# V's scratch in a decoder block with dilated attention: dense by head pair, the first group laid out by partition

## The chip, the cores and the metric

The kernel runs on one core of a Trainium2 chip. A core has TensorE (PE; its weight loads are shown apart, as PEld), VectorE (DVE), ScalarE (ACT), GpSimd (POOL) and SyncE (SP), which here only issues transfers. Sixteen DMA engines move data between the chip's memory (HBM) and the core's on-chip memory (SBUF). The metric is the device time of one execution in microseconds, the median of the runs.

## The reference, cut to what matters

One layer with sequence 2048 and width 1024. A combined projection gives q, k and v for three groups of eight heads of 64, and the inputs of a second branch. Each group attends to keys at a stride; the three outputs of a head slot are combined by their softmax denominators.

```python
DILATION_GROUPS = ((128, 1), (512, 4), (2048, 16))
...
proj = x @ w_in[l] + b_in[l]
q, k, v, g_attn, u_lru, g_lru, gate_logits = jnp.split(proj, SPLIT_POINTS, axis=-1)
...
for g, (window, dilation) in enumerate(DILATION_GROUPS):
    o_g, lse_g = dilated_band_attention(q[:, :, g], k[:, :, g], v[:, :, g], window, dilation)
...
y_a = attn @ w_attn_proj[l]
...
y_b = (h * jax.nn.silu(g_lru)) @ w_lru_proj[l]
merged = gates[:, :, 0] * y_a + gates[:, :, 1] * y_b
out = merged @ w_out[l] + b_out[l]
x = layer_norm(DEEPNORM_ALPHA * x + out, ln_gain[l], ln_bias[l])
```

In the attention each residue class of positions modulo the stride is cut into blocks of 128 queries, and each block sees its own keys and, in the first two groups, those of the block before.

## The kernel before, in words

The work runs in stages, one after the other on TensorE. The **projection** (to about 1452 us) computes the 72 feature tiles of 128 columns in two halves of the sequence, each half two chunks of 512 positions. Most pairs of tiles are made by seven products instead of eight (a Strassen form); `MID` is the order of the seven, and the results become complete at products 5, 2, 4 and 3, in that order: second tile in the half's second chunk, first tile in its first chunk, second tile in its first chunk, first tile in its second chunk. Every operand is split into a high and a low part in a reduced float format, and three matmuls stand for one. The **attention** (1452 to about 1791 us) takes 12 units, a unit being one group and one pair of heads, in the order group 0, 2, 1 within a head pair. It runs in 48 steps of four blocks, and the second branch's output projection (`yb`) is interleaved with it. The **output** stage follows.

The order on every engine is written by hand: what a Python loop emits is what each engine's queue holds, in that order. In the projection small generators (`chains`) emit the steps of each result some products later.

V's way is this. `v_chain` (L359) takes a finished tile of V with features in partitions, turns its four blocks of 128 positions with TensorE (L366), and ScalarE copies them from PSUM into one of two buffers `vs` (L374). SyncE stores the buffer to the scratch in HBM (L378). There are 48 such stores, 12 tiles by four chunks. The scratch `v_scr` (L50) has a tensor for each group and each two head pairs, with 260 floats a row: 130 for each head pair, of which the first and the last hold ones, set once in the buffers (L354 to L356). Nothing reads the ones.

In the attention `v_parts` (L799) gives the four loads of a unit: four blocks of 128 keys each, into one half of the tile `V` (L806), so that two units are there at a time. Group 0 takes consecutive keys to a block (L809), group 1 takes every fourth (L811), group 2 every sixteenth (L813); a load has 512 rows of 128 floats. The loads of unit u + 1 are emitted in steps 4u + 1 and 4u + 2 (L1282); those of unit 0 near the end of the projection (L869), those of unit 1 in step 1 (L1269). `values` (L1020) multiplies V with the turned weights.

SyncE's queue also carries q and k of the next unit (`qk_parts`, L794), the second branch's state `hx` (L1176), which GpSimd splits in `split_h` (L1180, L1181) before TensorE uses it in `yb_part` (L1205), its weights `wlr` (L1155), and small tensors, among them the weights `wh` of the groups (L1122), which `spread` multiplies in at L1129.

Of the kernel before, what the change touches and what calls it, by code (L numbers as in the profile page):

```python
# [8 lines left out]
F32 = mybir.dt.float32  # L9
F32R = mybir.dt.float32r  # L10
AF = mybir.ActivationFunctionType
# [4 lines left out]
P = 128  # L16
S = 2048
# [3 lines left out]
CH = 512  # L21
HP = 4
# [9 lines left out]
def hybrid_block_kernel(ctx: ExitStack, tc: tile.TileContext, a: dict, out: bass.AP):  # L32
    nc = tc.nc
    sp, act, dve, pool, pe = nc.sync, nc.scalar, nc.vector, nc.gpsimd, nc.tensor

    def flat(t):
        return t.bitcast(F32)


    dram = ctx.enter_context(tc.tile_pool(name="dram", bufs=1, space=DRAM))  # L40
# [6 lines left out]
    mg_scr = dram.tile([2 * D, S], F32, name="mg_scr")  # L47
    yb_scr = dram.tile([D, S], F32, name="yb_scr")

    v_scr = [[dram.tile([S, 260], F32, name=f"v_scr{g}{j}") for j in range(2)] for g in range(3)]  # L50

    qk_scr = {(n, u): dram.tile([P, S], F32, name=f"{n}_scr{u}") for u in range(12) for n in ("q", "k")}

# [48 lines left out]
    def big(slot, shape, dt, name):  # L102
        return (cur["Z"] if slot[0] == "Z" else X).tile(shape, dt, name=name, tag=slot)
# [8 lines left out]
    def pe_later(lag, fn):  # L112
        pe_late.append((now["n"] + lag, fn))
# [26 lines left out]
    sl_p = stA.enter_context(tc.tile_pool(name="sl_p", bufs=1))  # L140
# [15 lines left out]
    def give(*ts):  # L156
        for t in ts:
            vacant.append(home.pop(id(t))[0])
# [191 lines left out]
        give_sent(rp)  # L350


    vs_free = [sl_p.tile([P, 4, 130], F32, name=f"vs{j}") for j in range(2)]
    for t in vs_free:  # L354
        dve.memset(t[:, :, 0:1], 1.0)
        dve.memset(t[:, :, 129:130], 1.0)  # L356
    tog = {"n": 0}

    def v_chain(vt, sgn, f, c):  # L359
        g, hp = divmod(f - FT_V, 4)  # L360
        st = {}

        def turn():
            tp = st["tp"] = ps.tile([P, 4, P], F32, tag="t", name=f"vtp{f}_{c}", bufs=2)
            for b in range(4):
                pe.transpose(tp[:, b, :], flat(vt)[:, b * P:(b + 1) * P], ident)  # L366
            give(vt)

        yield Ask(cond=lambda: tog["n"] < 2)
        tog["n"] += 1  # L370
        pe_later(2, turn)
        yield Ask(lag=3, cond=lambda: len(vs_free) > 0, ACT=.66)
        vs = vs_free.pop(0)
        act.activation(vs[:, :, 1:129], st["tp"], AF.Copy, scale=sgn)  # L374
        tog["n"] -= 1
        yield Ask()
        dst = v_scr[g][hp // 2][c * CH:(c + 1) * CH, (hp % 2) * 130:(hp % 2) * 130 + 130]
        sp.dma_start(dst.rearrange("(b p) f -> p b f", p=P), vs)  # L378
        vs_free.append(vs)


# [199 lines left out]
    def result(s, fi, c, bank, u):  # L581
# [10 lines left out]
        if kind in ("qk", "v"):  # L592
            y = take("y" + nm)
            total(flat(y), bank, u, f, sgn, True)
            start_chain(qk_chain(y, f, c) if kind == "qk" else v_chain(y, sgn, f, c))
        elif kind == "mg":
            y = take("y" + nm, F32)
            total(y, bank, u, f, sgn, False)
            start_chain(mg_chain(y, sgn, f, c))
        elif kind == "ga" or not fi:  # L600
            y = take("y" + nm, F32)
            total(y, bank, u, f, sgn, False)
            start_chain(silu_chain(y, sgn, f, c))
        else:
            i = f - FT_U
            if c == 1 and i in put_off:
                y = take("y" + nm, F32)
                total(y, bank, u, f, sgn, True)
                act.activation(ubs[:, i, 2, 0:3], y[:, CH - 3:CH], AF.Copy)
                start_chain(store_chain(y, u_scr[i]))  # L610
                return
            ub = ub_free.pop(0)
            total(ub[:, 3:3 + CH], bank, u, f, sgn, True)
            start_chain(lru(i, c, ub), 7 if c % 2 else 0)
# [92 lines left out]
    for s, pl in enumerate(plan):  # L707
        if pl[0] and pl[4] == "ug":
            i = pl[1][1][0] - FT_U
# [71 lines left out]
    def unit(u):  # L781

        return (0, 2, 1)[u % 3], u // 3
# [14 lines left out]

    def v_parts(u):  # L799
        g, hp = unit(u)  # L800
        src = v_scr[g][hp // 2][:, 130 * (hp % 2) + 1:130 * (hp % 2) + 129]

        def part(i):
            def fn():
                if u == 0 and i == 0:
                    AT_X["v"] = big("X4", [P, 2, 16, P], F32, "V")  # L806
                V = AT_X["v"][:, u % 2, 4 * i:4 * i + 4]
                if g == 0:
                    sp.dma_start(V, src[i * CH:(i + 1) * CH].rearrange("(n p) f -> p n f", p=P))  # L809
                elif g == 1:  # L810
                    sp.dma_start(V, src[i * CH:(i + 1) * CH].rearrange("(j r) f -> j r f", r=4))  # L811
                else:
                    sp.dma_start(V, src.rearrange("(i r) f -> i r f", r=16)[:, 4 * i:4 * i + 4])  # L813
            return fn

        return [part(i) for i in range(4)]
# [48 lines left out]
    for t in sorted(early):  # L865
        for fn in early[t]:
            at(max(t, 0), fn)

    begin = {1: qk_parts(0), 3: v_parts(0), 5: qk_parts(1)}  # L869
    low = NS  # L870
    where = [(s, j) for s in range(NQ) for j in range(ticks[s])]
# [18 lines left out]
    n = len(where)  # L890
# [63 lines left out]
    st, ML = {}, {}  # L954
# [314 lines left out]
    for fn in v_parts(1):  # L1269
        at_group(1, fn)  # L1270
# [7 lines left out]
    for u in range(1, 11):  # L1278
        for i, fn in enumerate(qk_parts(u + 1)):
            at_group(4 * u + i // 2, fn)  # L1280
        for i, fn in enumerate(v_parts(u + 1)):
            at_group(4 * u + 1 + i // 2, fn)  # L1282
# [20 lines left out]
    for hp in range(3):  # L1303
        e = 4 * (3 * hp + 2) + 4
        for i in range(12):
            c, g = i // 3, (0, 2, 1)[i % 3]
# [3 lines left out]
    for G in range(NG + 1):  # L1310
# [30 lines left out]
        if y:  # L1341
            n, hf = divmod(halves[0], 2)
# [82 lines left out]
    for t in halves:  # L1425
        n, hf = divmod(t, 2)
# [139 lines left out]
    for t, tt in enumerate(TT):  # L1566
        c, b = divmod(t, 4)
# [67 lines left out]
```

## Time and profile before

| | |
|---|---|
| median of 3 runs | 2123.78 us (2121.55 to 2124.33) |
| the profiled execution | 2123.79 us |
| its span, first to last instruction | 2122.0 us |
| stores of V | 48 of 260 KB |
| loads of V | 48 of 256 KB |
| packets on SyncE's queue | 260688, 408.84 MB, 62.8% of 16 engines |
| memory read, written | 290.00 MB, 151.19 MB |

The profile is one execution on the chip. "Busy" for TensorE is the time in which a matmul is in flight; since matmuls are pipelined, a busy TensorE can still be slowed. Rows of waits give the engine and its line, what it waited for, the total in us, how many times, and the longest. A row of a timeline gives the start, the duration, the engine, the line and the tile, and in brackets the idle time before it with what ended it. A DMA's row on SyncE is the time to issue it; its data move later.

### The profile page before, as it was taken

The page shows a single profiled execution, that of the slowest core. Times are in us where ns is not written, and L with a number is a line of the kernel's source. Part 1 is how long each engine was busy: PE and PEld are TensorE (multiplying, and loading weights), DVE is VectorE, ACT ScalarE, POOL GpSimd, SP SyncE. Part 2 cuts the span into 40 slices and gives each one's busy share as a digit, 9 for nine tenths or more (in the row PEclk, how much of TensorE's full clock was granted, in tenths as well). Part 3 has the DMA queues.
Part 4 walks back from the last instruction along what each step waited for, and adds up shares of the span by engine and source line. Part 5 has one row for each costly group of instructions (what it writes and reads, how often), then busy time and mean ns, then how long its engine had stood idle before and what let it go on. Part 6 is the DMA issues. An engine that isn't in the chain of part 4 may idle for free. (4 is left out here: it accounts for less than half of the span.)

```text
span 2122.0 us, 34703 instructions
## 1 busy us (share of the span) xinstructions
PE 2099.0 (99%) x11637; PEld 1721.6 (81%) x11637; DVE 1660.3 (78%) x2938; ACT 1216.8 (57%) x2502; POOL 764.2 (36%) x692
## 2 busy tenths in 40 slices
PE   9999999999999999999999999999999999999998
PEld 7888888888888888888888888887878788788886
DVE  8787987988989767787677878775777777787667
ACT  6456456467457556677677777676666675321100
POOL 1554654654744301120110111113557678522120
PEclk9999999999999999999999999999999999999999
DMA  7876976976876966676666676769889886774431
GB/s 228 256 222 187 272 225 206 265 224 210 264 230 216 301 189 182 190 206 179 194 199 183 189 229 184 214 194 273 204 214 237 226 229 187 236 240 153 155 99 70
DMA packets 277505, 443.49 MB, mean 209 GB/s; under 512 B 64352, under 2 KB 116608, under 8 KB 274256
## 3 DMA queue, kind: packets, MB, share of 16 engines
q1 hardware_dynamic: 260688, 408.84, 62.8%
q0 software_dynamic: 11744, 23.54, 6.1%
q10 hardware_dynamic: 4896, 8.92, 1.1%
q8 instruction: 92, 1.51, 0.3%
q14 instruction: 85, 0.70, 0.1%
HBM read 290.00 MB, written 151.19 MB: 208 GB/s over the span
## 5 line engine op out<-in xcount | busy, mean ns | idle before, releaser
L633 PE MATMUL q<-xT,hS 128*128 128x512 f32 x1632 | 504.7, 390 | 0.0
L633 PE MATMUL q<-xT,l 128*128 128x512 f32 x1088 | 423.5, 389 | 0.0
L633 PE MATMUL q<-xB,hA 128*128 128x512 f32 x1344 | 417.2, 392 | 0.0
L633 PE MATMUL q<-xB,l 128*128 128x512 f32 x944 | 367.7, 389 | 0.0
L633 PEld LDWEIGHTS q<-xT,hS 128*128 128x128 f32 x1632 | 304.8, 188 | 64.4 <-issue 1.8
L633 PEld LDWEIGHTS q<-xB,hA 128*128 128x128 f32 x1344 | 250.3, 188 | 56.5 <-issue 5.5
L633 PEld LDWEIGHTS q<-xT,l 128*128 128x128 f32 x1088 | 204.3, 188 | 42.5
L236 POOL TENSOR_TENSOR sw<-sw,sin 128x512 f32<-128x512 f32 x96 | 156.1, 1632 | 167.7 <-ACT sw L325 74.0
L633 PEld LDWEIGHTS q<-xB,l 128*128 128x128 f32 x944 | 177.2, 188 | 37.0
L989 ACT ACTIVATE pt<-pt,ml 128x256 f32<-128x256 f32 (+1 forms) x384 | 172.2, 452 | 25.4 <-DVE ml L987 25.4
L236 POOL TENSOR_TENSOR y<-y,h 128x512 f32<-128x512 f32 x28 | 39.1, 1398 | 384.0 <-DVE h L535 368.0
L633 PE MATMUL q<-xB,hS 128*128 128x512 f32 x544 | 168.7, 391 | 1.1 <-DVE v L236 1.1
L633 PE MATMUL q<-xT,hA 128*128 128x512 f32 x544 | 167.9, 390 | 0.0
L280 ACT ACTIVATE hA<-wA 128x512 fp32r<-128x512 f32 x220 | 138.6, 635 | 29.2 <-DVE l L236 11.6
L1205 PE MATMUL yb<-hx,wl 128*128 128x512 f32 x576 | 149.5, 400 | 1.0 <-POOL hx L1181 0.8
L280 ACT ACTIVATE hS<-S 128x512 fp32r<-128x512 f32 x170 | 108.4, 638 | 66.0 <-DVE S L236 47.0
L236 POOL TENSOR_TENSOR l<-wA,hA 128x512 fp32r<-128x512 f32 x68 | 110.1, 1618 | 86.4 <-ACT hA L280 52.5
L1205 PEld LDWEIGHTS yb<-hx,wl 128*128 128x128 f32 x576 | 104.5, 188 | 29.9 <-issue 5.8
L987 DVE CUSTOM_DVE_ANT_0 pt<-s,mask 128x256 f32<-128x256 f32 (+1 forms) x384 | 115.6, 361 | 5.1 <-PE s L975 2.9
L633 PEld LDWEIGHTS q<-xT,hA 128*128 128x128 f32 x544 | 101.8, 188 | 21.7 <-issue 0.4
L633 PEld LDWEIGHTS q<-xB,hS 128*128 128x128 f32 x544 | 101.2, 188 | 22.4 <-issue 1.9
L324 ACT ACTIVATE sw<-y 64x512 f32<-64x512 f32 x96 | 60.6, 631 | 80.6 <-DVE y L577 78.7
(209 smaller groups left out, 4332.1 us busy)
## 6 DMA issues: line engine op xcount, KB each, us to landing
wA<-in_w_in_dram SPq DMA_DIRECT2D x220, 256.0 KB
wl_scr<-l SPq DMA_DIRECT2D x102, 512.0 KB
l<-wl_scr SPq DMA_DIRECT2D x102, 512.0 KB
wS<-in_w_in_dram SPq DMA_DIRECT2D x102, 256.0 KB
wS<-in_w_in_dram POOLq DMA_DIRECT2D x68, 256.0 KB, 6.8
wlr<-in_w_f_dram SPq DMA_DIRECT2D x64, 256.0 KB
mg_scr<-y SPq DMA_DIRECT2D x59, 256.0 KB
v_scr<-vs SPq DMA_DIRECT2D x48, 260.0 KB
```

Source lines behind the costliest of these rows:

```text
L236: eng.tensor_tensor(out=out, in0=in0, in1=in1, op=op)
L280: act.activation(heads(h), heads(r, False), AF.Copy)
L324: act.activation(flat(sw)[lo_], flat(rw)[up_], AF.Copy, scale=scale)
L633: pe.matmul(bank, w[:, ks], x[:, kk, xx], start=(first and i == 0), stop=(last and i == 11))
L987: dve.tensor_tensor_reduce(out=p[:, h, lo:256], in0=bank[h][:, m % 2, lo:256], in1=mask[:, lo:256], scale=1.0, scalar=3e38, op0=ALU.add, o ...
L989: act.activation(p[:, h, lo:256], p[:, h, lo:256], AF.Exp, scale=-1.0, bias=mm, accum_out=ll)
L1205: pe.matmul(YB["t"], w[:, a, k], hx(8 * c + k)[:, b], start=(hf == 0 and m == 0), stop=(hf == 1 and m == 11))
```

## The change

The scratch becomes twelve tensors, one for each group and head pair, of 2048 rows by 128 floats, without the columns of ones; the buffers `vs` lose those columns too, and the four instructions that set them are gone. For groups 1 and 2 row s holds position s, as before. For group 0 the rows are in the order partition, block: row 16 p + n holds position 128 n + p, so that a store writes 4 consecutive rows for each partition, and a load reads 4. In groups 1 and 2 the four rows that a partition takes in one load are consecutive positions, and now consecutive memory.

```diff
-    v_scr = [[dram.tile([S, 260], F32, name=f"v_scr{g}{j}") for j in range(2)] for g in range(3)]
+    v_scr = [[dram.tile([S, P], F32, name=f"v_scr{g}{j}") for j in range(HP)] for g in range(3)]
...
-    vs_free = [sl_p.tile([P, 4, 130], F32, name=f"vs{j}") for j in range(2)]
-    for t in vs_free:
-        dve.memset(t[:, :, 0:1], 1.0)
-        dve.memset(t[:, :, 129:130], 1.0)
+    vs_free = [sl_p.tile([P, 4, P], F32, name=f"vs{j}") for j in range(2)]
...
-        act.activation(vs[:, :, 1:129], st["tp"], AF.Copy, scale=sgn)
+        act.activation(vs, st["tp"], AF.Copy, scale=sgn)
...
-        dst = v_scr[g][hp // 2][c * CH:(c + 1) * CH, (hp % 2) * 130:(hp % 2) * 130 + 130]
-        sp.dma_start(dst.rearrange("(b p) f -> p b f", p=P), vs)
+        if g == 0:
+            sp.dma_start(v_scr[g][hp].rearrange("(p n) f -> p n f", p=P)[:, 4 * c:4 * c + 4], vs)
+        else:
+            sp.dma_start(v_scr[g][hp][c * CH:(c + 1) * CH].rearrange("(b p) f -> p b f", p=P), vs)
...
-        src = v_scr[g][hp // 2][:, 130 * (hp % 2) + 1:130 * (hp % 2) + 129]
+        src = v_scr[g][hp]
...
-                    sp.dma_start(V, src[i * CH:(i + 1) * CH].rearrange("(n p) f -> p n f", p=P))
+                    sp.dma_start(V, src.rearrange("(p n) f -> p n f", p=P)[:, 4 * i:4 * i + 4])
```

The loads of groups 1 and 2 keep their code: `"(j r) f -> j r f"` with r = 4, and `"(i r) f -> i r f"` with r = 16, four of the sixteen in each load.

## The prediction

> **What bounds the kernel now.** I read the page's head first, then busy time by stretches of the span, then what TensorE waited for.
>
> ```profile
> span 2122.0 us, 34703 instructions
> PE 2099.0 (99%) x11637; PEld 1721.6 (81%) x11637; DVE 1660.3 (78%) x2938; ACT 1216.8 (57%) x2502; POOL 764.2 (36%) x692
> DMA packets 277505, 443.49 MB, mean 209 GB/s; under 512 B 64352, under 2 KB 116608, under 8 KB 274256
> ```
>
> TensorE has work in flight for 2099.0 of 2122.0 us. Only 23.0 us of the span show it idle, and the change touches none of its 11637 matmuls. So the question is which of those 23 us hang on the V transfers. The profiled execution took 2123.79 us, 1.79 more than its span, and the median of the runs is 2123.78; I count from 2123.8.
>
> The stretches by stage (columns: width, then busy us and instructions of PE, PEld, DVE, ACT and POOL, granted clock, DMA share, GB/s):
>
> ```profile
> 1454.00:1486.00 32.00, 28.71 (x381) 22.90 (x379) 23.32 (x111) 26.69 (x109) 19.55 (x24) 1.00 1.05 285
> 1486.00:1791.00 305.00, 299.61 (x3354) 246.81 (x3353) 221.17 (x875) 205.48 (x798) 199.20 (x250) 1.00 0.83 217
> ...
> 2110.00:2122.00 12.00, 3.22 (x15) 2.33 (x13) 5.88 (x14) 0.29 (x1) 0.00 (x0) 0.78 0.12 44
> ```
>
> The attention stage, from 1454 to 1791, is where V is read. TensorE is idle there for 32.00 - 28.71 = 3.29 us at the start and 305.00 - 299.61 = 5.39 us in the rest. The tail after 2110 costs 8.78 us, and no V transfer is near it. The DMA engines are full at the start (1.05: packets overlap, so a share may pass 1) and at 0.83 afterwards, so a shorter transfer can only help in this stage, through whatever waits for data. TensorE's own waits, from the waits of that engine:
>
> ```profile
> PE first_bank L843 <- ACT warm L835: 3.2, 1, 3.2
> PE pt L1003 <- DVE o L236: 2.0, 2, 1.0
> PE pt L1003 <- ACT ptb L1016: 1.8, 3, 0.9
> PE q L633 <- DVE v L236: 1.1, 2, 0.8
> PE w L1129 <- DMA wh<-w_scr: 1.1, 1, 1.1
> ...
> PE yb L1205 <- POOL hx L1181: 0.8, 1, 0.8
> ```
>
> No wait names V. Two name something that shares V's queue: the weights wh, loaded through SyncE, and hx, which GpSimd splits after SyncE's load of it. The others belong to the start and to engines that hold their data already.
>
> **The stores and the columns of ones.** In the order: instruction, count, shortest, median and longest ns, first and last start.
>
> ```profile
> L374 ACT ACTIVATE vs<-vtp x48: 564/590/602, 116.8 to 1109.7; 128x512 f32<-128x512 f32 x48
> L378 SPq DMA_DIRECT2D v_scr<-vs x48: 370/385/1422, 117.4 to 1110.3; - x48
> L355 DVE MEMSET vs<- x2: 62/62/62, 1.4 to 1.4; 128x4 f32 x2
>   DMA v_scr<-vs: 16.4, 5
> ```
>
> The four memsets go (two at L355 and two alike at L356): 4 x 62 ns = 0.25 us of VectorE at 1.4 us. They lie behind the warm-up operands in program order, while TensorE waits 3.2 us for ScalarE's warm, so they are worth 0; without that cover, 0.25 us. The copy out of PSUM keeps its 512 elements per partition and only its output becomes contiguous. The trace shows no contiguous form of it: I bound it by its own spread, 26 ns less to 12 ns more than the median, so at most 48 x 0.026 = 1.2 us of ScalarE in either direction, beside 1000 us in which TensorE has matmuls queued. I take 0. The stores keep their 48 issues at 385 ns. Each of the 16 of the first group falls from 512 pieces of 520 B to 128 of 2 KB, the other 32 keep 512 pieces of 512 B. ScalarE waited 16.4 us in all for a store to leave its buffer; if every one of these waits went, ScalarE, busy 57% of the span, would stand idle for something else. Taken at 0, at most 1.1 us: that is all that TensorE's list shows of the projection, the wait for v at L236.
>
> **The loads.** There are 12 units of four loads each, 16 loads to a group; the rows of the three groups are alike, this is the first's.
>
> ```profile
> L809 SPq DMA_DIRECT2D V<-v_scr x16: 371/517/2722, 1441.8 to 1680.3; - x16
> ```
>
> The issues stay 48. What changes is their pieces: from 512 of 512 B to 128 of 2 KB, in all three groups. To price a piece I took two short stretches of the first units, one in which nearly all packets are V's 512 B, and one of 2 KB packets of other loads (first the stretch's row, then SyncE's queue in it: packets, MB, share of 16 engines; 0.84 MB in 1683 packets is 499 B each, 1.08 MB in 594 is 1818 B, completion marks included):
>
> ```profile
> 1448.50:1451.50 3.00, 3.00 (x15) 2.50 (x14) 1.28 (x2) 1.02 (x2) 0.54 (x1) 1.00 1.17 296
> q1 hardware_dynamic: 1683, 0.84, 111.1%
> 1461.70:1465.10 3.40, 3.40 (x54) 2.85 (x52) 3.05 (x13) 3.40 (x15) 0.00 (x0) 1.00 1.05 330
> q1 hardware_dynamic: 594, 1.08, 99.5%
> ```
>
> A unit of V is 4 x 256 KB = 1.049 MB. By rate it takes 1.049/296 = 3.54 us now and 1.049/330 = 3.18 us after: 0.36 us less. By the time of packets, one of 512 B takes 1.111 x 3.00 x 16/1683 = 32 ns, one of 2 KB 0.995 x 3.40 x 16/594 = 91 ns; a unit is 2048 x 32/16 = 4.1 us now and 512 x 91/16 = 2.9 us after: 1.2 us less. Packets overlap, so the rate is nearer to what a follower feels: I take 0.4 us per unit and keep 1.2 as the far end.
>
> [...]
>
> **Where a shorter unit is felt, first place.** SyncE's, GpSimd's and TensorE's timelines at the stage's start:
>
> ```profile
> 1452.75 5.70 SPq L1176 DMA_DIRECT2D hx<-hb_scr  x4
> ...
> 1466.34 0.61 POOL L1180 CAST hx<-hx 128x512 fp32r<-128x512 f32 x1 [11.17 <-DMA hx<-hb_scr]
> ...
> 1484.36 1.27 POOL L1181 TENSOR_TENSOR hx<-hx 128x512 fp32r<-128x512 f32 x1
> 1481.76 3.08 PE L1205 MATMUL yb<-hx,wl 128*128 128x512 f32 x10
> 1485.68 0.73 PE L1205 MATMUL yb<-hx,wl 128*128 128x512 f32 x2 [0.84 <-POOL hx L1181]
> ```
>
> GpSimd stands 11.17 us until the first hx lands; that load goes out at 1452.75, behind unit 0's V, whose loads are issued from 1441.8 on. From 1466.34 its splits follow each other without a pause, and the last one, ending 1485.63, releases TensorE after 0.84 us of idleness. If unit 0 is 0.4 us shorter, GpSimd starts 0.4 us earlier and TensorE's stall shrinks by 0.4 us (at the far end by all 0.84). Late next is ScalarE's copy ptb, which ends the other stalls here and doesn't move.
>
> **Second place.** The weights of the second head pair:
>
> ```profile
> 1654.75 1.25 SPq L811 DMA_DIRECT2D V<-v_scr x1
> ...
> 1659.05 1.55 SPq L1122 DMA_DIRECT2D wh<-w_scr  x4
> 1665.41 0.47 PE L1129 MATMUL w<-wh,sel 128*128 128x512 f32 x1 [1.09 <-DMA wh<-w_scr]
> ```
>
> The small wh loads go out behind a unit of V and TensorE waits 1.09 us for them. A unit shorter by 0.4 us gives 0.4 us, at the far end all 1.09. If the unit had drained before wh was issued, it gives 0.
>
> **Sum.** 0 (memsets, copies, stores) - 0.4 - 0.4 = -0.8 us: 2123.8 - 0.8 = **2123.0 us**. With the far ends, -0.84 - 1.09 = -1.9 us, and with the projection's 1.1 us -3.0 us: 2120.8; with no gain 2123.8.
>
> **The rivals.** *Nothing moves.* Units 2 to 11 are prefetched a whole unit ahead, the mean load of the queue is 0.83, and if both places wait for something that was issued earlier or runs at 296 GB/s as well, the shorter V ends in idle queue time: 2123.8. For it: TensorE's list has no V in it. Against: GpSimd's 11.17 us stand behind a full queue. [...]
>
> *The whole stage loosens.* If the full queue also delays what the list puts down to ScalarE and VectorE, each of the ten later units gives its 0.4 us of the 5.39 us idle: 2123.0 - 4.0 = 2119.0. For it: the share of 0.83 with 1.05 at the start. Against: these waits end on an engine's instruction, and their rows name ptb and o, which don't come by DMA.
>
> *A new wait on SyncE.* The first group's scratch is now written in interleaved rows, each chunk covering the address range of the three others. If the second store to a scratch waits until the first has landed, SyncE stands with weight loads behind it, in order, and ScalarE's and VectorE's splits and then TensorE wait for those. Each scratch gets two chunks in each half of the projection, so there are 4 x 2 = 8 such pairs. By the order of the products (5, 2, 4, 3 in MID) the first pair of the trace is this one:
>
> ```profile
> 119.39 0.38 SPq L378 DMA_DIRECT2D v_scr<-vs  x1
> ...
> 130.07 1.16 SPq L378 DMA_DIRECT2D v_scr<-vs  x1
> SPq L346 <- DVE y L236: 39.9, 11, 8.1
> ...
> SPq L346 <- DVE rp L236: 10.9, 4, 4.2
> ```
>
> It decides from the point at which a store takes over 130.07 - 119.39 = 10.7 us to land. Each such wait would cost TensorE about what a late operand costs it in the projection now, 0.8 us at most in its list: 8 x 0.8 = 6.4 us, 2130.2, slower by 0.30%. Against it: q's third group (L346) already writes interleaved slices of one scratch, and 15 of its 16 waits name VectorE's result, none an earlier store.
>
> **How the numbers follow.** A measurement of this kernel can tell about 0.2% from no change, which is 4.2 us. The forecast gets 0.55, nothing moves 0.30, the loosened stage 0.10, the new wait 0.05. The first two stay within 0.2%: same 0.85. The loosened stage is faster by 4.8 us, 0.23%: faster 0.10. Slower is the new wait: 0.05. The range begins at 2119.0, the loosened stage, which takes in 2120.8 from the unknown costs. Its upper end is nothing moves and one more stall of the longest seen in the middle of the stage, 1.1 us, and 0.6 us of the runs' spread above their median: 2125.5.
>
> **What would show it.** Right: packets fall by 24576 + 24576 - 16384 - 8192 = 24576 to about 252,900, nearly all of them from the class between 512 B and 2 KB; the first hx split starts 0.4 to 1.2 us before 1466.34 relative to the start of the stage; the stall for hx falls below 0.84; ScalarE's wait for v_scr falls. The tail and the projection keep their 8.78 us and their rows. Wrong: a wait of SyncE's store of V that names an earlier store of V; a first hx split that doesn't move, which says that the queue's rate is set elsewhere; a wait of TensorE on V; or a lower granted clock.

## The result and the profile after

| | before | after |
|---|---|---|
| median | 2123.59 us (2121.55 to 2124.33, 4 runs) | 2136.81 us (2136.23 to 2137.34, 4 runs) |
| ratio, 95% interval | | 1.0063 [1.0047, 1.0079] |
| the profiled execution | 2123.79 us | 2136.23 us |

The kernel became slower by 0.63%, 13.2 us. The prediction said 2123.0 us, with a range up to 2125.5.

The head of the page of after:

```profile
span 2134.4 us, 34699 instructions
PE 2113.6 (99%) x11637; PEld 1723.4 (81%) x11637; DVE 1660.9 (78%) x2934; ACT 1218.1 (57%) x2502; POOL 765.2 (36%) x692
DMA packets 252929, 443.30 MB, mean 208 GB/s; under 512 B 64352, under 2 KB 83840, under 8 KB 249680
```

The transfers did what was asked: 277505 - 252929 = 24576 packets fewer: 116608 - 83840 = 32768 fewer under 2 KB and 8192 more of 2 KB. But TensorE is busy for 2113.6 us instead of 2099.0, with the same 11637 matmuls. TensorE's waits in after, complete:

```profile
PE first_bank L842 <- ACT warm L834: 3.2, 1, 3.2
PE pt L1002 <- DVE o L236: 2.0, 2, 1.0
PE pt L1002 <- ACT ptb L1015: 1.8, 3, 0.9
PE ya L1477 <- DVE at L1376: 1.1, 1, 1.1
PE w L1128 <- ACT ptb L1015: 0.9, 1, 0.9
PE w L1128 <- DVE o L236: 0.5, 1, 0.5
PE pt L1002 <- ACT pt L988: 0.4, 2, 0.2
```

The stalls for wh and for hx are gone from the list, and no new wait of 13 us stands in it (the one of 1.1 us for `at` is new; it comes up again below). So the time isn't in a wait; TensorE works longer. The stretches tell where. First before (columns: width, then busy us and instructions of PE, PEld, DVE, ACT and POOL, granted clock, DMA share, GB/s), a stretch of the projection and one of the output stage:

```profile
500.00:600.00 100.00, 100.00 (x443) 82.84 (x442) 86.32 (x101) 59.89 (x96) 58.25 (x41) 1.00 0.79 242
1950.00:2050.00 100.00, 100.00 (x443) 82.81 (x442) 71.62 (x116) 10.94 (x17) 20.14 (x12) 1.00 0.42 137
```

Then after, with the attention's two stretches as the prediction set them (15 us later) and the tail:

```profile
500.00:600.00 100.00, 100.00 (x436) 81.72 (x435) 87.30 (x103) 58.36 (x94) 57.22 (x40) 1.00 0.79 240
1950.00:2050.00 100.00, 100.00 (x443) 82.78 (x442) 72.57 (x123) 10.97 (x17) 16.60 (x10) 1.00 0.40 135
1469.00:1501.00 32.00, 29.70 (x411) 24.39 (x409) 24.39 (x116) 26.87 (x110) 21.38 (x26) 1.00 1.00 294
1501.00:1806.00 305.00, 300.70 (x3339) 248.02 (x3336) 222.59 (x872) 205.65 (x798) 200.40 (x252) 1.00 0.79 217
2122.40:2134.40 12.00, 3.23 (x15) 2.34 (x13) 5.88 (x14) 0.29 (x1) 0.00 (x0) 0.77 0.12 44
```

In the projection TensorE starts 436 matmuls in 100 us instead of 443, at a granted clock of 1.00 in both, and is "busy" for the whole of both stretches. The output stage runs at the old pace of 443, and the tail is the same. The count of instructions is what shows the loss; the busy time of a stretch that is full in both kernels can't. The busy time of the weight loads does fall, from 82.84 to 81.72 us, where TensorE's is 100.00 twice.

One row of a group says it of all matmuls of a kind, here the largest of the projection, in before and then in after:

```profile
L633 PE MATMUL q<-xT,hS 128*128 128x512 f32 x1632 | 504.7, 390 | 0.0
```

```profile
L632 PE MATMUL q<-xT,hS 128*128 128x512 f32 x1632 | 508.0, 392 | 0.0
```

The end of the projection, from TensorE's timeline, is where the last product's matmul (q) gives way to the first of the attention (s). Before:

```profile
1452.31 0.39 PE L633 MATMUL q<-xB,l 128*128 128x512 f32 x1
1452.62 0.38 PE L975 MATMUL s<-qk 64*128 64x128 f32 x2
```

After:

```profile
1466.90 0.40 PE L632 MATMUL q<-xB,l 128*128 128x512 f32 x1
1467.23 0.38 PE L974 MATMUL s<-qk 64*128 64x128 f32 x2
```

The projection lost 1467.23 - 1452.62 = 14.61 us. What follows it is shorter: 2122.0 - 1452.62 = 669.38 us became 2134.4 - 1467.23 = 667.17, 2.21 less. Of that the attention's stretches hold 3.29 - 2.30 = 0.99 and 5.39 - 4.30 = 1.09 us less idleness of TensorE. Loss and gain together are 12.4 us, the difference of the spans. Only the loss is clear of the spread between single executions: in nine kernels with the old loads of V (before and those of the experiments below, without e11 and its stall) the part behind the projection takes 667.8 to 670.7 us.

A matmul's own duration, 390 and 392 ns in these rows, runs on over the next one's start, so I took the time from one start to the next. The projection does three matmuls with each pair of operands: high with high, high with low, low with high. In before they follow each other at 226 to 227 ns; in after, in the blocks of x that did not change their place, at 232, 226 and 229 ns. With 6096 matmuls of 128x512 in the projection, 14.61 us are 2.4 ns for each on the mean.

What could slow matmuls that the change doesn't touch? The buffers `vs`. Each shrank from 4 x 130 to 4 x 128 floats per partition, 2080 to 2048 B, and there are two. All that is allocated behind them in the same pool moves 64 B down: the slots that hold the projection's split weights (the stationary operand), and the last block of x (the `xB` with the highest number). The other blocks of x (the moving operand) are allocated ahead and stay. By the tiles' addresses in the program, the weights and the x of a matmul start a multiple of 256 B apart within a partition in before (x from byte 19872, the slots behind the buffers from 131488: 111616 = 436 x 256). In after 5024 of the 6096 matmuls are 64 B short of that. The others have the last block of x, which moved along, or weights in the one slot that lies ahead of the buffers; 1040 of them keep their multiple of 256 B.

### The profile page after: what moved, and what is told of

Read it like the earlier page. It is cut to its first block, busy times and chain, and to the rows that moved or that the text cites. A ratio compares the mean times of both kernels' runs of the same rounds, so it can differ in the third digit from the quotient of the medians.

```text
span 2134.4 us, 34699 instructions
## 1 busy us (share of the span) xinstructions
PE 2113.6 (99%) x11637; PEld 1723.4 (81%) x11637; DVE 1660.9 (78%) x2934; ACT 1218.1 (57%) x2502; POOL 765.2 (36%) x692
## 2 busy tenths in 40 slices
DMA packets 252929, 443.30 MB, mean 208 GB/s; under 512 B 64352, under 2 KB 83840, under 8 KB 249680
## 5 line engine op out<-in xcount | busy, mean ns | idle before, releaser
L280 ACT ACTIVATE hS<-S 128x512 fp32r<-128x512 f32 x170 | 108.4, 638 | 70.8 <-DVE S L236 55.6
```

What stands on the lines that cost most here:

```text
L280: act.activation(heads(h), heads(r, False), AF.Copy)
```

## The experiments

The theory was that the distance between the two operands in SBUF sets the pace. Its rivals: the new store or load transfers disturb the operands' splits or TensorE; the narrower buffers matter by themselves; the weights' absolute place matters. "Distance" below is weights' address minus x's, modulo 256 B; before has 0, after 192. Where a single time stands, it is one run beside before's in the same series.

**The change with the old buffers** (e1), against after. The transfers, the scratch and the contiguous copy stay new; only the buffer's size goes back. Distance 0.

```diff
-    vs_free = [sl_p.tile([P, 4, P], F32, name=f"vs{j}") for j in range(2)]
+    vs_free = [sl_p.tile([P, 520], F32, name=f"vs{j}")[:, 0:CH].rearrange("p (b f) -> p b f", f=P) for j in range(2)]
```

> The changed kernel, whole, but each of the two store buffers takes its old 2080 B per partition (the last 32 B unused), so every tile behind them lies where it lay before. Place (the slots of the projection's weights moved by 64 B, and each projection matmul is about 2.5 ns slower for it): back to 2121 to 2124 us, 457 to 459 matmuls between 100 and 200 us, and what is left of the DMA change shows as the 0 to 3 us of my prediction. Transfers (2 KB pieces or the new scratch slow TensorE): 2134 to 2138 us, 454 to 455 matmuls there.

Measured: 2123.28 us (11 runs) against 2124.84 (15 runs), ratio 0.9996 [0.9987, 1.0005]. The whole loss is gone. The projection has before's pace again (459 matmuls between 100 and 200 us, where before has 458 and after 455), and the projection ends at before's time:

```profile
500.00:600.00 100.00, 100.00 (x443) 82.81 (x442) 87.03 (x101) 60.01 (x95) 58.35 (x41) 1.00 0.79 239
1454.00:1486.00 32.00, 28.48 (x380) 22.40 (x376) 23.18 (x109) 26.54 (x109) 19.04 (x23) 1.00 1.03 296
1486.00:1791.00 305.00, 299.84 (x3355) 247.38 (x3356) 221.10 (x876) 205.63 (x798) 199.63 (x252) 1.00 0.79 216
```

```profile
1452.16 0.39 PE L632 MATMUL q<-xB,l 128*128 128x512 f32 x1
1452.48 0.38 PE L974 MATMUL s<-qk 64*128 64x128 f32 x2
```

This run also gives the worth of the transfers alone: 0.04% less with an interval of 0.09% to either side, that is nothing that can be told in the whole time. The attention's idleness, 32.00 - 28.48 = 3.52 and 305.00 - 299.84 = 5.16 us, sums to 8.68 as it did before.

**The old scratch with the new buffers** (e2), against before: the reverse. The loads and the scratch stay old, the ones are left out (nothing reads them). Distance 192.

```diff
-    vs_free = [sl_p.tile([P, 4, 130], F32, name=f"vs{j}") for j in range(2)]
+    vs_free = [sl_p.tile([P, 4, P], F32, name=f"vs{j}") for j in range(2)]
...
-        dst = v_scr[g][hp // 2][c * CH:(c + 1) * CH, (hp % 2) * 130:(hp % 2) * 130 + 130]
+        dst = v_scr[g][hp // 2][c * CH:(c + 1) * CH, (hp % 2) * 130 + 1:(hp % 2) * 130 + 129]
```

> The kernel before with only the store buffers changed: 2048 B per partition, no columns of ones, stored into the old scratch of 260 floats a row; all loads of V stay 512 pieces of 512 B. Place: 2134 to 2138 us, 454 to 455 matmuls between 100 and 200 us. Transfers: 2121 to 2124 us, 457 to 459.

Measured: 2139.81 us (4 runs) against 2124.84, ratio 1.007 [1.0056, 1.0084], and 454 matmuls between 100 and 200 us. The projection ends late without any of the new loads:

```profile
1466.54 0.40 PE L630 MATMUL q<-xB,l 128*128 128x512 f32 x1
1466.87 0.38 PE L972 MATMUL s<-qk 64*128 64x128 f32 x2
```

So the loads are out as a cause. The stores and the copy are still in both slow kernels; the next ones take them out.

**64 B more ahead of the buffers** (e3), against before, with all of before's code. Distance 64.

```diff
+    pad = sl_p.tile([P, 16], F32, name="pad")
+    dve.memset(pad, 0.0)
     vs_free = [sl_p.tile([P, 4, 130], F32, name=f"vs{j}") for j in range(2)]
```

> The kernel before with 64 B per partition put in ahead of the store buffers: the weights' slots lie 64 B further on instead of 64 B back, the blocks of x stay. If the offset within 128 B decides (96 instead of 32, as in the changed kernel): 2134 to 2138 us. If the offset within 256 B or more decides: another time than both, anywhere from 2110 to 2140. If nothing about the place matters: 2121 to 2124.

Measured: 2154.23 us against 2124.84. A pad that nothing reads costs 29 us, twice the change's loss, at the same granted clock:

```profile
500.00:600.00 100.00, 100.00 (x433) 80.68 (x431) 89.45 (x106) 59.73 (x95) 56.37 (x40) 1.00 0.79 239
1950.00:2050.00 100.00, 100.00 (x443) 82.84 (x442) 71.27 (x124) 13.18 (x20) 19.12 (x12) 1.00 0.46 153
```

433 matmuls in the projection's stretch, 443 in the output's, which the pad doesn't touch.

**x moved along instead of back** (e4), against after: 64 B ahead of everything, so that the weights lie where they lay in before, to the byte, and x lies 64 B higher. Distance still 192.

```diff
     lr = cst.tile([P, 8, 8], F32, name="lr")
+    pad = cst.tile([P, 16], F32, name="pad")
+    dve.memset(pad, 0.0)
```

> The changed kernel with 64 B put in ahead of the blocks of x and of everything behind them: the weights' slots are back at the offset of before, the blocks of x lie 64 B further on. If the weights' own offset decides, the projection has 457 to 459 matmuls between 100 and 200 us (2121 to 2124 us, apart from the later stages, which now have all their tiles moved by 64 B and may slow). If the offset between weights and x decides, it stays at 454 to 455.

Measured: 2137.11 us, 454 matmuls between 100 and 200 us. The weights' own address is not it. **The same pad in before** (e9) moves x and weights together, distance 0:

> The kernel before with 64 B put in ahead of the blocks of x and everything behind them: x and the weights' slots both move by 64 B, their distance stays a multiple of 256 B. If the distance decides: 2121 to 2125 us and 443 matmuls between 500 and 600 us. If the places themselves decide (an offset of 160 B within 256 being the good one for both): 2135 to 2157 us.

Measured: 2124.61 us against 2122.68 (15 runs from 2120.16 to 2125.25), within that spread, and the projection's stretch has its 443 matmuls:

```profile
500.00:600.00 100.00, 100.00 (x443) 82.78 (x442) 87.66 (x103) 60.21 (x95) 58.12 (x41) 1.00 0.79 239
```

**Other sizes of the pad of e3**: 128, 256, 512, 32 and 192 B (32, 64, 128, 8 and 48 floats), each in before.

> The kernel before with 128 B put in ahead of the store buffers, so that the weights' slots lie 128 B further on from x. Distance with a period of 128 B: 2121 to 2125 us and 226.7 ns from matmul to matmul in the projection. A longer period: another time, by the 64 B runs some 10 to 30 us more.

> The same with 256 B. Distance with a period of 256 B or less: 2121 to 2125 us. A longer period: another time.

> The same with 512 B, the length of one weight tile per partition. Distance with a period of 512 B or less: 2121 to 2125 us, as in the kernel before, where weights and x differ by a multiple of 512 B. If instead only a multiple of 1024 or 2048 B is free of loss: 2130 to 2155 us.

> The same with 32 B, half of the 64 B that cost 30 us. If the loss grows with the distance up to 64 B: 2135 to 2145 us. If 64 B is the grain and 32 B stays inside it: 2121 to 2125 us. If anything but the same offset loses all: 2150 to 2156 us.

> The kernel before with 192 B put in ahead of the store buffers. If only the distance within 256 B matters, this is the changed kernel's distance (64 B back is 192 B on): 2133 to 2139 us, with its pattern of 232, 226 and 229 ns in the projection. If every distance but a multiple of 256 B costs according to its size: 2150 to 2160 us, like 32, 64 and 128 B.

Measured, with the rest beside them (matmuls started between 500 and 600 us from the windows of each kernel):

| distance mod 256 B | kernels | us | matmuls in 500 to 600 |
|---|---|---|---|
| 0 | before; e1; pads of 256 and 512 B; e9 | 2121.26 to 2124.84; 2123.28; 2120.31, 2121.47; 2124.61 | 443 |
| 32 | pad of 32 B | 2156.72 | 431 |
| 64 | pad of 64 B | 2154.23 | 433 |
| 128 | pad of 128 B | 2156.57 | 432 |
| 192 | after; e2; e4; pad of 192 B | 2136.81; 2139.81; 2137.11; 2136.85 | 436 or 437 |

The pad of 192 B is a move up by 192, the change a move down by 64: the same distance modulo 256, the same time, and the same 232, 226 and 229 ns from start to start. The pads of 256 and 512 B cost nothing (2120.31 and 2121.47 us beside 2121.26): in these runs the distance counts modulo 256 B. One row of each tells the pads of 256 and of 192 B apart, the first free, the second slow:

```profile
500.00:600.00 100.00, 100.00 (x443) 82.85 (x442) 88.02 (x102) 60.02 (x95) 58.55 (x41) 1.00 0.80 244
```

```profile
500.00:600.00 100.00, 100.00 (x436) 81.70 (x435) 86.08 (x101) 58.41 (x95) 57.14 (x40) 1.00 0.77 238
```

**The same in another stage** (e11), against before: 64 B ahead of the memory of attention and output, so that in six of eight pairs of operands of the last product `z` the activations lie 64 B off the weights. The projection is as before.

```diff
     w_p = stC.enter_context(tc.tile_pool(name="w_p", bufs=1, reuse_waits="tile"))
+    pad = Z.tile([P, 16], F32, name="pad", tag="zpad")
+    dve.memset(pad, 0.0)
     OT = [big(f"Z{i}", [P, 2, S], F32, f"o{i}") for i in range(3)]
```

> The kernel before with 64 B put in ahead of the second half of the memory that the attention and the output stages use: in the output stage the stationary operand ms then lies 64 B further on from those parts of the output weights that lie in the first half (6 of 8), at a time when the DMA engines are 0.39 busy and ScalarE 11%. Distance between TensorE's two operands: the matmuls z take 2 to 6 ns more (229 to 233 ns instead of 227 on average), the attention's o and pt may slow as well, in all 2 to 8 us: 2123 to 2131 us. Collisions with what other engines and transfers write to the slots: z stays at 226.7 ns, 2121 to 2125 us. The projection keeps its 443 matmuls between 500 and 600 us in either case.

Measured: 2136.01 us against 2122.68, more than expected, for two reasons that the trace keeps apart. The projection keeps its pace; `z` is slow; and the pad's memset is a stall of its own. From the windows of this kernel and, behind them, the last stretch's row of before (it holds `z` and, between its parts, `ya`):

```profile
500.00:600.00 100.00, 100.00 (x442) 82.78 (x442) 87.97 (x103) 60.17 (x96) 58.26 (x41) 1.00 0.79 242
1400.00:1500.00 100.00, 87.73 (x678) 72.27 (x677) 59.34 (x178) 56.71 (x166) 36.27 (x47) 0.93 0.80 225
1900.00:2100.00 200.00, 200.00 (x867) 162.32 (x867) 139.81 (x228) 22.42 (x33) 39.23 (x24) 1.00 0.39 129
```

```profile
1900.00:2100.00 200.00, 200.00 (x884) 165.62 (x883) 141.39 (x238) 22.67 (x34) 35.71 (x22) 1.00 0.39 129
```

867 matmuls where before has 884.

VectorE's timeline, the memset with the idle time before it in brackets:

```profile
1463.08 0.07 DVE L911 MEMSET pad<- 128x16 f32 x1 [10.87 <-DMA mg_scr<-y]
```

TensorE's waits:

```profile
PE pt L1005 <- ACT pt L991: 10.9, 1, 10.9
```

The memset waited for memory that the projection's last results still held, and VectorE, ScalarE and TensorE stood behind it for 10.9 us; the granted clock's mean fell to 0.93 in that stretch. That stall is the memset's and says nothing of the distance. The distance shows beside it: from start to start the 768 matmuls of `z` take 232.5 ns in the mean instead of 226.7, 768 x 5.8 = 4.5 us. By pairs, 575 matmuls with operands 64 B off take 233.3 ns, 192 with operands a multiple of 256 B apart 230.1 ns. In the two profiles the first `z` starts 7.4 us later than in before, so 3.5 us of the long stall are made up by then, and from there to the end of `z` 4.8 us more are lost: 12.2 us, the difference of the spans. That `z` slows shows that the effect is not the projection's own.

**The identity's place** (e12), against e1: the tile that TensorE uses to turn blocks lay 32 B off (modulo 256) the tiles that it turns; `b72` is allocated ahead of it, which sets that distance to 0.

```diff
+    b72 = cst.tile([P, 72], F32, name="b72")
     ident = cst.tile([P, P], F32, name="ident")
...
-    b72 = cst.tile([P, 72], F32, name="b72")
```

> The changed kernel with the old buffer size, and the identity matrix placed a multiple of 256 B from the tiles that TensorE turns with it (it lay 32 B off in all kernels so far). Distance: the 1200 small turns of the attention and the 192 of V lose 1 to 4 ns each, 1 to 5 us in all: 2116 to 2122 us, faster than the kernel before. If so small operands don't feel it: 2121 to 2124 us, as the changed kernel with old buffers.

Measured: 2123.82 us (11 runs) against before's 2122.68 (15 runs), ratio 1.0001 [0.9992, 1.001]. The 1200 turns of 64 columns, first in e1, then here:

```profile
L1002 PE MATMUL pt<-ident,pt 64*128 64x64 f32 x1200 | 56.5, 227 | 5.7 <-DVE o L236 2.0 <-ACT ptb L1015 1.8 <-ACT pt L988 0.4
```

```profile
L1002 PE MATMUL pt<-ident,pt 64*128 64x64 f32 x1200 | 56.7, 228 | 5.7 <-DVE o L236 2.0 <-ACT ptb L1015 1.6 <-ACT pt L988 0.4
```

Nothing moved, from start to start either (31.3 ns in the mean in both; the 192 turns of V, of 128 columns, 108.4 in both): no loss was measured in these short matmuls at a distance of 32 B, and there was no gain to be had there. No kernel of the series beat before by more than a measurement can tell (the lowest, 2120.31 with a pad of 256 B, is one run beside 2121.26).

## Why the prediction was wrong

**The step that failed** is the one at its start: "Only 23.0 us of the span show it idle, and the change touches none of its 11637 matmuls. So the question is which of those 23 us hang on the V transfers." That took the 2099.0 busy us as fixed because the instructions are the same. The buffer edit was priced by its memsets, its copy and its stores, at 0, and not by what it moves: 32 B less for each buffer moved the projection's weights by 64 B and took 5056 of its 6096 matmuls off their multiple of 256 B. Shown: e1 gives only the size back and the loss goes; e3 changes only the place and makes a loss; e9 moves both operands and makes none. At 14.61 us it outweighs every term of the sum. No rival had it either; the one on the slower side was a wait.

**Packets**: right. About 252,900 were forecast, 252929 came. The loads' issues fell as well; the median for the first group, 517 ns before, is 382 after:

```profile
L808 SPq DMA_DIRECT2D V<-v_scr x16: 325/382/584, 1456.3 to 1693.8; - x16
```

**The first place (hx)**: no gain shown. With the projection at its old pace (e1) GpSimd's first split starts later than before, not earlier, from its timeline:

```profile
1466.85 0.61 POOL L1179 CAST hx<-hx 128x512 fp32r<-128x512 f32 x1 [11.83 <-DMA hx<-hb_scr]
```

1466.85 - 1452.48 = 14.37 us after the start of the stage, where before has 1466.34 - 1452.62 = 13.72. SyncE's timeline and, last, its waits around the start of the stage in e1:

```profile
1441.70 1.79 SPq L808 DMA_DIRECT2D V<-v_scr  x4
...
1452.89 6.66 SPq L1175 DMA_DIRECT2D hx<-hb_scr  x4
```

```profile
SPq L793 <- DMA qk<-k_scr: 4.6, 2, 2.7
```

The four loads of V are issued in 1.79 us, where before needs 4.40, but SyncE's loads of q and k (L793) then wait twice, 4.6 us in all, for an earlier load of k to land, which before's don't, and hx still goes out at 1452.9 (1452.75 before). V was not what kept it. In after the first split, from GpSimd's timeline, stands here:

```profile
1479.43 0.61 POOL L1179 CAST hx<-hx 128x512 fp32r<-128x512 f32 x1 [9.65 <-DMA hx<-hb_scr]
```

That is 12.20 us after the stage's start and 1.5 us earlier than before, and the stall is gone. Neither the transfers nor the slow projection explain it: e4 has both, and its first split comes at 14.1 us with stalls of 1.0 us for hx. The nine kernels with the old loads lie between 13.4 and 14.5 us, e12 at 13.7. After's one profile stands alone, and why is open.

**The second place (wh)**: not shown either, though e1 looks right to the size. From TensorE's waits in e1:

```profile
PE yb L1204 <- POOL hx L1180: 1.2, 2, 0.9
PE ya L1477 <- DVE at L1376: 1.2, 1, 1.2
...
PE w L1128 <- DMA wh<-w_scr: 0.7, 1, 0.7
```

The stall for wh is 0.7 us where before has 1.09, a fall of the forecast 0.4. But with the old loads the same stall is 0 to 1.4 us from one kernel's profile to the next (none in e9, 1.4 with the pad of 128 B), and with the new ones none in after, e4 and e12. The fall in e1 is inside that spread, so its agreement is luck.

**Where the shorter V went.** TensorE reaches the first matmul of `ya`, in the output stage, 395.7 to 396.9 us after the attention's start in the four kernels with the new transfers (after, e1, e4, e12), and 397.4 to 400.3 us after it in the nine with the old loads. The means differ by 1.8 us, more than the 0.8 of the sum; each kernel has one profile, and which waits gave it is not shown. Then the four stand 1.1 to 1.2 us for VectorE's `at`, as e1's row above and after's list show; with the old loads that stall is at most 0.6. VectorE's splits of `at` stand there behind a step that waits for a load of its own (`vec`, 1.29 us in e1). At the end of those `ya` the means are 0.5 us apart and the two ranges overlap. The prediction followed the gain to a stall in the attention and not on to the next stage. In the whole time nothing is left that can be told, 0.9996 in e1 and 1.0001 in e12, and these intervals can't tell -0.8 us from the rival "nothing moves".

**The rate of the pieces** was set too low. In e1, two stretches in which V's pieces of 2 KB fill the queue:

```profile
1448.50:1450.50 2.00, 2.00 (x10) 1.65 (x9) 0.64 (x2) 0.15 (x1) 0.54 (x1) 1.00 1.05 355
1464.50:1466.00 1.50, 1.50 (x34) 1.33 (x32) 1.50 (x10) 1.50 (x7) 0.00 (x0) 1.00 1.05 385
```

355 and 385 GB/s, where 330 was taken from other loads and the 512-B pieces have 296. The window of 330 was a slow one: before's other loads, most of them 2 KB pieces too, reach 393 GB/s between 1464.5 and 1466 us. By these rates a unit is shorter by 17 to 23%, more than the 10% in the sum.

**The rival of a new wait on SyncE**: not seen. The stores' waits in after name ScalarE's copy alone, none an earlier store:

```profile
SPq L377 <- ACT vs L371: 20.3, 9, 5.0
SPq L375 <- ACT vs L371: 18.2, 7, 5.0
```

**The contiguous copy**, in the order shortest, median and longest ns, in after:

```profile
L371 ACT ACTIVATE vs<-vtp x48: 566/587/603, 118.7 to 1118.8; 128x512 f32<-128x512 f32 x48
```

587 ns in the median against 590: 0, as taken. **The tail** kept its 12.00 - 3.23 = 8.77 us. Of the signs of being wrong that the prediction named, a wait on a store, a wait on V and a lower clock stayed away; the fourth, a first hx split that doesn't come earlier, is what e1 and e4 show. Of the signs of being right, ScalarE's wait for `v_scr` did not fall clearly: 16.4 us before, 12.7 in after, 17.3 in e1. That the projection keeps its rows was named as well, and it did not; but the prediction put no price on it, and none of its signs of being wrong looked at the pace of the matmuls.

## What to carry to other kernels

In this kernel a change of a buffer's size was also a change of the place of everything allocated behind it; before such an edit is priced, list those tiles and ask which engine reads two of them at once. When a kernel bound by TensorE gets slower and no wait has grown, count the matmuls in equal stretches (443 against 436 here): the stage in which the count falls is the one to look at; its busy time, 100.00 us in both here, did not show it. With the weights and the moving operand a multiple of 256 B apart in a partition, 443 of this kernel's matmuls of 128x512 fell into 100 us; at 32, 64, 128 and 192 B it was 431 to 437. So look at that distance where such matmuls stand back to back, or pad a buffer that shrinks to its old size: e1 does it with 32 B each and takes 2123.28 us where after takes 2136.81. And before one stall's change is put down to an edit, look at the same stall in kernels that don't have the edit: here the stall for wh ranges from 0 to 1.4 us among kernels with the old loads, more than the forecast gain of 0.4.

## What the runs showed of the hardware

- In before, where the two operands lie a multiple of 256 B apart in SBUF, matmuls of 128x512 in this kernel's split float format follow each other at 226 to 227 ns. At 192 B modulo 256 (after and the pad of 192 B) they come at 232, 226 and 229 ns in the pattern of the projection's three; at 32, 64 and 128 B (the pads of those sizes) at 233 in the mean, 431 to 433 in 100 us against before's 443. Over the kernel that is 12 to 15 us at 192 and 29 to 35 us at the others, with the granted clock at 1.00 in the stretches compared.
- Matmuls that kept their multiple of 256 B were slow too among others that had lost it. The last block of x moved along with the weights in after, so its own distance stayed right in 72 of its 76 products. Its twelve matmuls of a product still begin slow and settle, while a block that stayed keeps its pattern (ns from start to start, mean of 76 products of the first and 68 of one other, without the places where TensorE did other work in between):

```
block that moved along: 233 231 232 234 226 230 233 228 231 230 228 227
block that stayed:      231 227 230 232 227 230 231 227 229 231 226 230
```

  In before all twelve are at 226 to 227. The 192 matmuls of `z` in e11 with the right distance, among others with a wrong one, are slow too, at 230.1 ns. From these times I estimate that a delay is carried into matmuls that wouldn't cause one; the times are shown, the carrying is not.
- Turns of 64 columns (31.3 ns from start to start in both e1 and e12) did not react to a distance of 32 B.
- TensorE's pace depends here on the places of both operands together: 64 B between x and the weights (e3) took 2154.23 us, 64 B ahead of both (e9) 2124.61. With the same matmuls the kernel took 2120 to 2125 us or 2154 to 2157 by nothing but the place of one operand against the other.
- Why the loss is gone at 256 and 512 B, and why 192 B costs less than 32, 64 and 128 (2136.85 us against 2156.72, 2154.23 and 2156.57), no run here shows. That is left open, as are other data types and the sizes between those tried.
